# The end of a causal depthwise convolution: how many taps are left over before the last group's input, and how the last group's 31 taps are shared among four engines

## The chip, the core and the metric

The kernel runs on one core of a Trainium2 chip. A core has five engines that run their own instruction queues in order and meet at semaphores: TensorE (PE, with its weight loads PEld), VectorE (DVE), ScalarE (ACT), GpSimd (POOL) and SyncE (SP), which here issues the loads. The metric is the device time of one execution in microseconds, the median of several runs; beside it stands one execution that the hardware profiler recorded, with start and length of every instruction.

## The reference

The kernel computes a trunk of two layers on 256 tokens of width 2048, in float32. Layer 0 mixes tokens with a convolution module, layer 1 with latent attention; each is followed by a squared-ReLU MLP of width 8192. The change lies in the convolution module alone:

```python
def conv_module(h, w_pw1, b_pw1, w_dw, b_dw, ln_g, ln_b, w_pw2, b_pw2):
    u = h @ w_pw1 + b_pw1
    a, gate = jnp.split(u, 2, axis=-1)
    u = a * jax.nn.sigmoid(gate)
    u = lax.conv_general_dilated(          # depthwise, causal, width 31
        u, w_dw[:, None, :].astype(u.dtype), window_strides=(1,),
        padding=[(CONV_WIDTH - 1, 0)],
        dimension_numbers=("NWC", "WIO", "NWC"),
        feature_group_count=D_MODEL) + b_dw
    u = jax.nn.silu(layer_norm(u, ln_g, ln_b))
    return u @ w_pw2 + b_pw2
```

The depthwise convolution is, for each of the 2048 channels, a sum of 31 products: tap `w` is the channel's weight `w_dw[w]` times the gated input shifted by `w` tokens. The LayerNorm behind it needs all channels of a token, so nothing of the second projection can start before the last channel's sum is done.

## The kernel before

The 2048 channels are worked in 16 groups (`KC`) of 128, group `c` from 0 to 15. A group's gated input is a tile of 128 channels by 256 tokens with 30 zeros ahead (`ub`).

**One step of the loop.** A written-out loop (`for c in range(1, KC + 1)`) holds the order; the program says in which order each engine gets its instructions. In step `c` PE works on the first projection for group `c` (`conv_mm`, three passes of split float32), while the other engines finish group `c - 1`: `glu(c - 1)` forms the gated input from the projection's two accumulators, `start_sum` begins its sum of taps, `dve_taps` works through taps, `side_sum` adds up side products. Weights are split into a high and a low part by `conv_half(n, h)`: ACT writes `hi` (L173), and GpSimd or DVE writes `lo` (L174) from it; piece `n` of the weights has two halves. `conv_load` issues the load of a piece on SP's queue; there are three raw buffers, and a load waits until both halves of the piece three before it are split.

**Who computes a tap.** A tap can be done in three ways:
- DVE: one fused multiply and add onto an accumulator in PSUM (`dve_tap`, L978).
- Side tap: ACT multiplies (`product`, L898), GpSimd adds the products up in a tree (`side_sum`, L954), and DVE adds the tree's result to the accumulator (the join, an entry `None` in the list, L961).
- PE, in the last two groups only: ACT writes a diagonal matrix of the tap's 128 weights (`diag`, L907), and PE multiplies it by the shifted input (`last_products`, L918; `but_one_products`, L926 for group 14). `LAST_PE` taps of group 15 are done so, in two halves, eight of group 14.

**Leftovers.** `left[c]` is the list of a group's DVE taps that are not yet done. `dve_taps(c)` takes taps, oldest group first and in turn from two groups, until the number left over all groups is down to `rest(c)`: `REST` in general, `LAST_REST` for groups 13, 14 and 15. The taps left over are done in the next step. In the last step (`c == KC`, group 15) nothing may be left. Group 15's gated input `ub` is written by DVE itself (L888), and so stands in DVE's queue behind the taps of `dve_taps(14)`.

**The last step.** PE: the eight products of group 14, the first half of `last_products`, the transposes of group 13 to token order (`to_tokens`, L1016, which `dve_taps` issues when group 13's last tap has been issued), the second half, eight warm-up transposes (`keep_warm`, L238), the transposes of groups 14 and 15, 26 more warm-up transposes. DVE: the remaining taps; `half` (L972), the last tap of groups 14 and 15; `ca` (L975), which adds PE's part to `half`. `fill` holds the two statistics of groups 12 and 13 (`ln_stats`, L1026), put between the taps once `n` has reached `FILL_AT[1]` = 15 in the last step, otherwise behind them. Then: statistics of groups 14 and 15, mean and variance, reciprocal root (`rsqrt`, L221 to L226, whose square root runs on ACT), normalisation (L1159), swish and the second projection.

**Buffers.** The diagonals have `LAST_PE` buffers of 128 floats a partition, the side products `sum(LAST_SIDE)` buffers of 256.

Of the kernel before, what the change touches and what calls it, by code (L numbers as in the profile page):

```python
# [20 lines left out]
KC = D // P  # L21
# [23 lines left out]
PAD_O = 16  # L45
WB = 6
LOOK = WB // 2 - 1
LAST_PE = 22
BUT_ONE_PE = 8
SIDE = 2  # L50
LAST_SIDE = (3, 6, 4)
JOIN = 14
LEAD = 7
REST = (16, 18, 22)
LAST_REST = (20, 9, 0)
FILL_AT = (5, 15)
ORDERS = "STSTSTOSTSTSTSTT", "TSTSTSTOSTSTSTST"
N_S, N_G = 9, 2
# [28 lines left out]
def trunk_kernel(  # L87
# [55 lines left out]
    def nm(s):  # L143
        uid[0] += 1
        return f"{s}_{uid[0]}"


    def acc_tile():
        return psum["acc"].tile([P, NB], F32, tag="acc", name=nm("acc"))
# [17 lines left out]
    def split_half(raw, h, eng):  # L167

        _, nj, cols = raw.shape
        js = slice(h * nj // 2, (h + 1) * nj // 2)  # L170
        hi = wpool.tile([P, nj // 2, cols], F32R, tag="hi", name=nm("hi"), bufs=WB)
        lo = wpool.tile([P, nj // 2, cols], F32R, tag="lo", name=nm("lo"), bufs=WB)
        nc.scalar.activation(hi, raw[:, js, :], AF.Copy)  # L173
        eng.tensor_tensor(lo, raw[:, js, :], hi.bitcast(F32), op=ALU.subtract)  # L174
        return hi, lo
# [628 lines left out]
    with ExitStack() as cx:  # L804
# [30 lines left out]
        def conv_load(n):  # L835
            if n < NU:
                c, k = n // UC, n % UC * 8
                raws[n] = load(
                    [rows(conv_w_pw1[0], k, 8, c * P, P), rows(conv_w_pw1[0], k, 8, D + c * P, P)], 8
                )  # L840
            elif n < NU + KC // 2:
                raws[n] = load([rows(conv_w_pw2[0], 2 * (n - NU), 2, 0, 2 * NB)], 2)

        def conv_half(n, h):
            if n < NU + KC // 2:
                wjs[n, h] = split_half(raws[n], h, nc.gpsimd if 0 < n + h and (n, h) < (NU + 1, 1) else nc.vector)
# [20 lines left out]
        pss, ubs, pcs, cas, cts, sides, left = {}, {}, {}, {}, {}, {}, {}  # L867
        rest = lambda c: LAST_REST[c - KC + 3] if c > KC - 4 else REST[min(c, 2)]
        n_side = lambda c: LAST_SIDE[c - KC + 3] if c > KC - 4 else SIDE
        tap = lambda c, w: w_dw[:, w * KC + c : w * KC + c + 1]  # L870
# [9 lines left out]
        def glu(c):  # L880
            ub = ubs[c] = cv2.tile([P, PAD + S], F32, tag="ub", name=nm("ub"), bufs=3)
            (nc.vector if c == KC - 1 else nc.gpsimd).memset(ub[:, 0:PAD], 0.0)
            sg = cv2.tile([P, S], F32, tag="sg", name=nm("sg"), bufs=1)
            va, ga = pss.pop(c)
            nc.scalar.activation(sg, ga[:, :S], AF.Sigmoid, bias=b_pw1[:, KC + c : KC + c + 1])
            if c == KC - 1:

                nc.vector.scalar_tensor_tensor(  # L888
                    out=ub[:, PAD:], in0=va[:, :S], scalar=b_pw1[:, c : c + 1], in1=sg, op0=ALU.add, op1=ALU.mult
                )  # L890
            else:
                vb = cv2.tile([P, S], F32, tag="vb", name=nm("vb"), bufs=1)
                nc.scalar.activation(vb, va[:, :S], AF.Identity, bias=b_pw1[:, c : c + 1])
                nc.gpsimd.tensor_tensor(ub[:, PAD:], vb, sg, op=ALU.mult)

        def product(c, w):
            pr = cv2.tile([P, S], F32, tag="tp", name=nm("tp"), bufs=sum(LAST_SIDE))
            nc.scalar.activation(pr, ubs[c][:, w : w + S], AF.Copy, scale=tap(c, w))  # L898
            return pr

        def diag(c, w):
            if c == KC - 2:
                t, j = divmod(w - W + BUT_ONE_PE, 4)
                dg = cn[:, t, (KC - 4 + j) * P : (KC - 3 + j) * P]
            else:
                dg = cv2.tile([P, P], F32, tag="dg", name=nm("dg"), bufs=LAST_PE)
            nc.scalar.activation(dg, ident, AF.Copy, scale=tap(c, w))  # L907
            return dg
# [7 lines left out]
        def last_products(w0, w1):  # L916
            for w in range(w0, w1):
                nc.tensor.matmul(  # L918
                    last_sum[0], dgs[w], ubs[KC - 1][:, w : w + S], start=w == 0, stop=w == LAST_PE - 1
                )  # L920

        def but_one_products():
            but_one_sum.append(acc_tile()[:, :S])
            for i, dg in enumerate(but_one):
                w = W - BUT_ONE_PE + i
                nc.tensor.matmul(  # L926
                    but_one_sum[0], dg, ubs[KC - 2][:, w : w + S], start=i == 0, stop=i == BUT_ONE_PE - 1
                )

        def start_sum(c):  # L930
# [7 lines left out]
            else:  # L938
                pcs[c] = acc_tile()[:, :S]
                o = sum_tile()[:, :S]  # L940
                last_sum.append(o)
                last_products(0, LAST_PE // 2)
                w = LAST_PE
            n = n_side(c)
# [4 lines left out]
        def side_sum(c):  # L949
            ps = sides[c]  # L950
            step = 1
            while step < len(ps):
                for i in range(0, len(ps) - step, 2 * step):
                    nc.gpsimd.tensor_tensor(ps[i], ps[i], ps[i + step], op=ALU.add)  # L954
                step *= 2

        def dve_tap(c):
            w = left[c].pop(0)
            out = pcs[c]
            if w is None:  # L960
                nc.vector.tensor_tensor(out, out, sides[c][0], op=ALU.add)  # L961
                return
            if c == KC - 1 and w == LAST_PE + n_side(c):
                nc.vector.tensor_scalar(
# [17 lines left out]
        def dve_taps(c, fill):  # L982
# [4 lines left out]
            while sum(len(v) for v in left.values()) > rest(c):  # L987
# [12 lines left out]
                if c == KC - 1 and k == KC - 3 and not left[k]:  # L1000

                    to_tokens(k)
                    last_products(LAST_PE // 2, LAST_PE)
                last = turns["last"] = k
# [4 lines left out]
        def to_tokens(c):  # L1009

            if c % 2 == 0:
                cts[c // 2] = acc_tile() if c == KC - 2 else tr_tile()
            ct = cts[c // 2]
            for t in range(T):
                q = 2 * t + c % 2
                nc.tensor.transpose(  # L1016
                    ct[:, q * P : (q + 1) * P], ca_part(c)[:, t * P : (t + 1) * P], ident
                )

        def ln_stats(c):  # L1020
            fill = []
            if c % 2 == 1:
                ct = cts[c // 2]
                for t in range(T):
                    fill.append(
                        lambda t=t: nc.vector.bn_stats(stats[:, t, c // 2, :], ct[:, t * S : (t + 1) * S])  # L1026
                    )
                fill.append(lambda: nc.scalar.activation(
                    cn[:, :, (c - 1) * P : (c + 1) * P], ct.rearrange("p (t n) -> p t n", t=T), AF.Copy
                ))  # L1030
            return fill
# [11 lines left out]
        with tc.manual_schedule():  # L1043
# [57 lines left out]
            for c in range(1, KC + 1):  # L1101
                n = UC * c
                conv_load(n + 3)
                if c == KC:
                    but_one_products()
                glu(c - 1)
                fill = ln_stats(c - 4 if c < KC else KC - 3) if c > 3 else []
                fill, copies = fill[:T], fill[T:]
                if c < KC:
                    pss[c] = [acc_tile() for _ in range(2)]  # L1110
                conv_half(n + (c < KC), 0)
                start_sum(c - 1)
                if c < KC:
                    conv_half(n + 1, 1)
                    dve_taps(c - 1, fill)
                    conv_load(n + 4)
                    side_sum(c - 1)
                    conv_mm(c, 0, 8)
                    if c < KC - 1:
                        conv_half(n + 2, 0)  # L1120
                        conv_half(n + 2, 1)
                else:
                    side_sum(c - 1)
                    conv_half(n, 1)
                    conv_half(n + 1, 0)
                    dve_taps(c - 1, fill)
                    conv_load(n + 4)
                for f in copies:
                    f()
                if c < KC:  # L1130
                    conv_mm(c, 8)
                    if c > KC - 4:
                        dgs.extend(diag(KC - 1, w) for w in range(len(dgs), min(len(dgs) + 8, LAST_PE)))
                    if c == KC - 1:
                        but_one.extend(diag(KC - 2, w) for w in range(W - BUT_ONE_PE, W))
                    if c > 2:
                        to_tokens(c - 3)
                    conv_mm(c, 12)
# [139 lines left out]
    with ExitStack() as cx:  # L1278
# [322 lines left out]
        with tc.manual_schedule():  # L1601
# [89 lines left out]
            for g in range(NG):  # L1691
                for i in range(HG):
                    h = g * HG + i

                    n = -(-len(work) // (HG - i))
# [116 lines left out]
```

## Time and profile before

| what | value |
|---|---|
| median of 3 runs | 1931.16 us (1931.03 to 1931.22) |
| profiled execution, its own time | 1930.93 us |
| its span, first to last instruction | 1929.2 us |
| granted TensorE clock | 0.998 |
| busy: PE, DVE, ACT, POOL | 1904.2, 1647.4, 1208.2, 223.4 us |
| convolution's last two steps | about 190 to 217 us of the span |

In the profile, times are microseconds from the span's start. A row of a timeline has start, length, engine, line, operation, output and inputs with their shapes, the number of merged instructions, and in brackets the idle time of the engine ahead of it and who ended it. The lengths of neighbours on an engine overlap, so the step from one start to the next is what an instruction costs in a row of them. A row of the chain of waits has start, length and what the end of the program was waiting for then. `tr`, `acc` and `sum` are PSUM tiles; `tp` are side products, `dg` diagonals, `ca` a finished group.

### The profile page before, as it was taken

Reading aid. Unit: us, or ns where it says so; the run is one execution under the profiler, and the core shown is the slowest. Engines: PE = TensorE matmul, PEld = TensorE weight load, DVE = VectorE, ACT = ScalarE, POOL = GpSimd, SP = SyncE. Lnnn points to the kernel's source line nnn. Section 1 sums busy time; section 2 is a strip of 40 time slices with the busy share of each in tenths; the row PEclk is TensorE's granted clock in tenths of the full one; section 3 lists DMA queues with packets and bytes.
Section 4 is the critical chain, followed back from the end, with each engine's and each line's share of the span. In section 5 each row is a group of like instructions: output and inputs, shape, how many; then the busy total and the mean of one; then the engine's idle time right before and its main releaser. Section 6 shows DMA issues by size and latency. Waiting matters only on the chain.

```text
span 1929.2 us, 28511 instructions
## 1 busy us (share of the span) xinstructions
PE 1904.2 (99%) x10794; PEld 1669.2 (87%) x10794; DVE 1647.4 (85%) x2367; ACT 1208.2 (63%) x1717; POOL 223.4 (12%) x183
## 2 busy tenths in 40 slices
PE   7999999999999999999999999999999999999998
PEld 7999888888888888888899998888888888888886
DVE  5999865789999999999976665657999999999887
ACT  5556664766666666666566665566666666666654
POOL 5999300000000000000001410000000000000000
PEclk9999999999999999999999999999999999999999
DMA  8676365857666667666646445765667666766663
GB/s 236 187 195 179 129 196 154 234 172 206 203 201 206 197 202 213 200 200 212 205 143 182 118 151 175 205 188 173 199 193 210 208 197 197 217 201 197 212 220 109
DMA packets 407113, 367.62 MB, mean 191 GB/s; under 512 B 15416, under 2 KB 351936, under 8 KB 406720
## 3 DMA queue, kind: packets, MB, share of 16 engines
q1 hardware_dynamic: 405952, 363.63, 63.0%
q10 hardware_dynamic: 1024, 2.17, 0.3%
q8 instruction: 84, 1.38, 0.3%
q14 instruction: 53, 0.43, 0.1%
HBM read 363.68 MB, written 2.10 MB: 190 GB/s over the span
## 4 chain that ended last, share of the span: by engine, by line
PE 88%; DVE 9%; ACT 1%; POOL 1%; DMA 0%; issue 0%; SPq 0%; DVEq 0%; ACTq 0%; POOLq 0%
PE acc L520 24%; PE acc L199 15%; PE acc L200 15%; PE acc L201 15%; PE acc L518 12%; DVE sum L978 7%; PE acc L255 1%; PE sum L918 1%; ACT hi L173 0%; DMA xs<-in_x 0%; PE acc L863 0%; PE acc L864 0%; PE acc L865 0%; PE acc L1580 0%; PE acc L1444 0%
## 5 line engine op out<-in xcount | busy, mean ns | idle before, releaser
L431 DVE TENSOR_TENSOR lo<-raw,hi 128x1024 fp32r<-128x1024 f32 (+1 forms) x512 | 571.7, 1123 | 88.0 <-ACT hi L430 87.6
L430 ACT ACTIVATE hi<-raw 128x1024 fp32r<-128x1024 f32 (+1 forms) x512 | 480.0, 971 | 66.0 <-PE acc L200 65.8
L520 PE MATMUL acc<-xt,hi 128*128 128x512 f32 x2048 | 504.0, 391 | 0.0
L520 PEld LDWEIGHTS acc<-xt,hi 128*128 128x128 f32 x2048 | 374.8, 188 | 72.8 <-ACT hi L430 0.2
L199 PE MATMUL acc<-hi,sh 128*128 128x512 f32 x930 | 362.7, 390 | 0.0
L201 PE MATMUL acc<-lo,sh 128*128 128x512 f32 x930 | 361.9, 389 | 0.0
L200 PE MATMUL acc<-hi,sl 128*128 128x512 f32 x802 | 312.0, 389 | 0.0
L518 PEld LDWEIGHTS acc<-xt,lo 128*128 128x128 f32 x2048 | 257.7, 188 | 10.9
L518 PE MATMUL acc<-xt,lo 128*128 128x256 f32 x2048 | 259.7, 279 | 0.0
L173 ACT ACTIVATE hi<-raw 128x1024 fp32r<-128x1024 f32 (+2 forms) x184 | 180.1, 1006 | 46.2 <-PE acc L200 43.3
L201 PEld LDWEIGHTS acc<-lo,sh 128*128 128x128 f32 x930 | 174.5, 188 | 36.3
L199 PEld LDWEIGHTS acc<-hi,sh 128*128 128x128 f32 x930 | 174.6, 188 | 35.9
L174 DVE TENSOR_TENSOR lo<-raw,hi 128x1024 fp32r<-128x1024 f32 (+2 forms) x118 | 132.9, 1146 | 68.3 <-ACT hi L173 62.3
L430 ACT ACTIVATE hi<-V 128x1024 fp32r<-128x1024 f32 x94 | 99.6, 1060 | 130.7 <-DVE V L726 121.7
L200 PEld LDWEIGHTS acc<-hi,sl 128*128 128x128 f32 x802 | 150.5, 188 | 31.3
L978 DVE SCALAR_TENSOR_TENSOR sum<-ub,w_dw,sum 128x256 f32<-128x256 f32 x392 | 160.0, 512 | 6.4 <-ACT sum L934 5.5
L174 POOL TENSOR_TENSOR lo<-raw,hi 128x1024 fp32r<-128x1024 f32 x66 | 157.7, 2407 | 23.7 <-ACT hi L173 23.1
L430 ACT ACTIVATE hi<-T 128x1024 fp32r<-128x1024 f32 x94 | 99.5, 1058 | 92.5 <-DVE T L714 68.9
L525 ACT ACTIVATE U<-acc 128x512 f32<-128x512 f32 x128 | 75.9, 593 | 108.6 <-PE acc L520 108.6
L863 PE MATMUL acc<-xt,hi 128*128 128x256 f32 x512 | 143.6, 280 | 0.0
L865 PE MATMUL acc<-xt,lo 128*128 128x256 f32 x512 | 142.2, 278 | 0.6 <-POOL lo L174 0.6
L864 PE MATMUL acc<-xt,hi 128*128 128x256 f32 x512 | 142.2, 278 | 0.0
(275 smaller groups left out, 2810.4 us busy)
## 6 DMA issues: line engine op xcount, KB each, us to landing
raw<-in_mlp_w SPq DMA_DIRECT2D x256, 1024.0 KB, 6.2
raw<-in_conv_w_pw SPq DMA_DIRECT2D x64, 512.0 KB, 5.5
raw<-in_conv_w_pw SPq DMA_DIRECT2D x16, 1024.0 KB, 5.0
raw<-in_mla_w_o SPq DMA_DIRECT2D x16, 1024.0 KB, 5.5
raw<-in_mla_w_kv_up SPq DMA_DIRECT2D x8, 1024.0 KB, 5.6
raw<-in_mla_w_in SPq DMA_DIRECT2D x8, 576.0 KB, 3.8
raw<-in_mla_w_in SPq DMA_DIRECT2D x4, 1024.0 KB, 6.0
raw<-in_mla_w_q_up SPq DMA_DIRECT2D x16, 256.0 KB, 3.8
```

The lines of the kernel that those rows point to most:

```text
L173: nc.scalar.activation(hi, raw[:, js, :], AF.Copy)
L174: eng.tensor_tensor(lo, raw[:, js, :], hi.bitcast(F32), op=ALU.subtract)
L199: nc.tensor.matmul(ps, sh, mh, start=start, stop=False)
L200: nc.tensor.matmul(ps, sl, mh, start=False, stop=False)
L201: nc.tensor.matmul(ps, sh, ml, start=False, stop=stop)
L430: nc.scalar.activation(parts[0], src, AF.Copy)
L431: nc.vector.tensor_tensor(parts[1], src, parts[0].bitcast(F32), op=ALU.subtract)
L518: nc.tensor.matmul(ps[0][:, :S], wl[:, j, :], xh(k), start=False, stop=False)
L520: nc.tensor.matmul(ps[0], wh[:, j, :], xhl(k), start=k == 0, stop=k == KC - 1)
L863: nc.tensor.matmul(o, wh[:, bs], xh(k), start=k == 0, stop=False)
L864: nc.tensor.matmul(o, wh[:, bs], xl(k), start=False, stop=False)
L978: nc.vector.scalar_tensor_tensor(out=out, in0=ubs[c][:, w : w + S], scalar=tap(c, w), in1=pcs[c], op0=ALU.mult, op1=ALU.add)
```

## The change

Three numbers and the place of one call change:
- `LAST_PE` 22 to 18: PE does 18 of group 15's taps.
- `LAST_SIDE[2]` 4 to 6: six of group 15's taps go through ACT and GpSimd. DVE is left with 31 - 18 - 6 = 7 and the join, where it had 31 - 22 - 4 = 5 and the join.
- `LAST_REST[1]` 9 to 16: `dve_taps(14)` stops with 16 entries left over instead of 9.
- In the last step the first `conv_half(n, 0)`, a split of a piece of the second projection's weights, moves from ahead of `start_sum` to behind `side_sum`. In the other steps the call stays where it was.

```diff
-LAST_PE = 22
+LAST_PE = 18
 BUT_ONE_PE = 8
 SIDE = 2
-LAST_SIDE = (3, 6, 4)
+LAST_SIDE = (3, 6, 6)
 JOIN = 14
 LEAD = 7
 REST = (16, 18, 22)
-LAST_REST = (20, 9, 0)
+LAST_REST = (20, 16, 0)
 FILL_AT = (5, 15)
...
-                conv_half(n + (c < KC), 0)
+                if c < KC:
+                    conv_half(n + 1, 0)
                 start_sum(c - 1)
                 if c < KC:
                     conv_half(n + 1, 1)
...
                 else:
                     side_sum(c - 1)
+                    conv_half(n, 0)
                     conv_half(n, 1)
                     conv_half(n + 1, 0)
                     dve_taps(c - 1, fill)
```

The buffers of the diagonals go from 22 to 18, those of the side products from 13 to 15.

## The prediction

> **What bounds the kernel now.** I read the page first: its head, the engines' busy time and the chain that ended last.
>
> ```profile
> span 1929.2 us, 28511 instructions
> ...
> PE 1904.2 (99%) x10794; PEld 1669.2 (87%) x10794; DVE 1647.4 (85%) x2367; ACT 1208.2 (63%) x1717; POOL 223.4 (12%) x183
> ...
> PE 88%; DVE 9%; ACT 1%; POOL 1%; DMA 0%; issue 0%; SPq 0%; DVEq 0%; ACTq 0%; POOLq 0%
> ```
>
> TensorE (PE) carries 88% of the chain. DVE has 9%, nearly all of it in the convolution, where the taps (`dve_tap`, L978) set the pace. The change edits only the last two of the convolution's 16 channel groups, so next comes the chain of waits there, in order of time (start, us, what):
>
> ```profile
> 197.09 8.24 DVE sum L978 x21
> 205.33 0.41 DVE ub L888
> ...
> 205.78 5.02 PE sum L918 x22
> 210.80 0.22 PE tr L1016 x2
> 211.02 4.75 PE sum L918 x22
> 215.77 0.87 PE acc L238 x8
> 216.64 0.45 PE acc L1016 x4
> ...
> 217.12 0.76 DVE stats L1026 x2
> ...
> 218.79 0.49 ACT cn L1028
> ```
>
> Until 205.3 the chain is DVE's taps of groups 13 and 14. Behind them in DVE's queue stands `ub` of group 15 (L888), which everything of the last group needs. Then PE's 22 diagonal products (two instructions each, in halves of 22, the transposes of group 13 between them) run to 215.77; then come warm-up transposes (L238), the transposes of groups 14 and 15, the LayerNorm statistics, the root on ScalarE (ACT), and the second projection. The timelines of DVE and PE tell how much room each has:
>
> ```profile
> 205.21 0.51 DVE L888 SCALAR_TENSOR_TENSOR ub<-acc,vecs_cv,sg 128x256 f32<-128x256 f32 x1
> ...
> 205.58 1.33 DVE L978 SCALAR_TENSOR_TENSOR sum<-ub,w_dw,sum 128x256 f32<-128x256 f32 x3
> ...
> 207.53 0.61 DVE L964 TENSOR_SCALAR acc<-ub,w_dw,vecs_cv 128x256 f32<-128x256 f32 x1
> 207.98 0.55 DVE L978 SCALAR_TENSOR_TENSOR sum<-ub,w_dw,sum 128x256 f32<-128x256 f32 x1
> ...
> 210.27 0.55 DVE L972 SCALAR_TENSOR_TENSOR half<-ub,w_dw,sum 128x256 f32<-128x256 f32 x1
> 210.91 0.42 DVE L975 TENSOR_TENSOR ca<-acc,half 128x256 f32<-128x256 f32 x1
> ...
> 211.59 0.42 DVE L1026 BATCH_NORM_STATS2 stats<-tr 128x6 f32<-128x256 f32 x1
> 211.93 0.46 DVE L972 SCALAR_TENSOR_TENSOR half<-ub,w_dw,acc 128x256 f32<-128x256 f32 x1
> 215.81 0.42 DVE L975 TENSOR_TENSOR ca<-sum,half 128x256 f32<-128x256 f32 x1 [3.42 <-PE sum L918]
> ```
> ```profile
> 201.31 3.61 PE L926 MATMUL acc<-ub,cn 128*128 128x256 f32 x16
> 205.78 5.02 PE L918 MATMUL sum<-ub,dg 128*128 128x256 f32 x22 [0.86 <-DVE ub L888]
> ```
>
> So PE waits 0.86 for `ub` at 205, and DVE waits 3.42 for PE at the end of the group. The two are out of balance by that much, and the change shifts work from PE to DVE.
>
> **The change part by part.**
>
> *16 taps left over instead of 9.* Seven taps of groups 13 and 14 move from before `ub` to behind it. 21 alternating taps take 8.24 us in the chain, 0.393 each; `ub` comes 7 x 0.393 = 2.75 earlier, its start at 202.46. What else it needs is there: the gate's sigmoid starts at 201.57 (row below) and lasts 0.47. PE cannot take all of this: its 16 products of group 14 run from 201.31, 3.61 long, to 204.92. An L918 starts every (210.63 - 205.78) / 22 = 0.22 us, the end of one overlapping the next, so without the wait the next starts at about 204.8. PE gains 0.9 to 1.0 there; the other 1.8 of the 2.75 is hidden behind PE.
>
> *18 taps on PE instead of 22.* Four products, eight instructions of 0.22, fall away: 1.76 us, four in each half. First half 204.8 + 18 x 0.22 = 208.77; transposes of group 13 start there; second half from 208.99 to 213.0, against 215.7. PE's part shrinks by 2.7. The four diagonals that ACT no longer makes were ahead of the sigmoid:
>
> ```profile
> 197.24 1.85 ACT L907 ACTIVATE dg<-ident,w_dw 128x128 f32<-128x128 f32 x6
> ...
> 201.57 0.47 ACT L885 ACTIVATE sg<-acc,vecs_cv 128x256 f32<-128x256 f32 x1
> ...
> 205.76 1.71 ACT L898 ACTIVATE tp<-ub,w_dw 128x256 f32<-128x256 f32 x4 [2.77 <-DVE ub L888]
> ...
> 216.69 0.60 ACT L1028 ACTIVATE cn<-tr 128x512 f32<-128x512 f32 x1 [7.32 <-DVE stats L1026]
> 217.29 1.28 ACT L232 ACT_TABLE_LOAD   x1
> ```
>
> That is 1.2 us of ACT, but the sigmoid waits for PE's last gated product (201.31 is where PE goes on to L926), so it is worth 0 to 0.1; I take 0.
>
> *Six side taps on ACT and GpSimd, and the weight split (`conv_half(n, 0)`) behind them.* `ub` ends at 202.97. Six products at 0.42 (the L898 row: four in 1.71) end at 205.6. GpSimd (POOL) now has five additions instead of three, and the moved half's conversion comes after them:
>
> ```profile
> 203.07 2.35 POOL L174 TENSOR_TENSOR lo<-raw,hi 128x1024 fp32r<-128x1024 f32 x1 [0.84 <-ACT hi L173]
> 206.75 2.33 POOL L954 TENSOR_TENSOR tp<-tp,tp 128x256 f32<-128x256 f32 x3 [1.33 <-ACT tp L898]
> 209.04 4.67 POOL L174 TENSOR_TENSOR lo<-raw,hi 128x1024 fp32r<-128x1024 f32 x2
> ```
>
> The additions start 1.0 behind `ub` as here, at 204.0, at 0.75 to 0.8 each with the waits for products: last one done at 207.9. DVE's join wants it at 213.4 (below), so that costs nothing; without that cover each late us would be one us at the end. Then three conversions at 2.34: 210.2, 212.5, 214.9 (before: 213.7). All feed the second projection, which begins behind 218: hidden. The second frees a buffer for a 1 MB load on SP's queue, 1.1 later than now; at the page's 5.0 us it lands near 217.6, and ACT converts that piece from about 229:
>
> ```profile
> raw<-in_conv_w_pw SPq DMA_DIRECT2D x16, 1024.0 KB, 5.0
> ```
> ```profile
> 231.75 2.00 ACT L173 ACTIVATE hi<-raw 128x1024 fp32r<-128x1024 f32 x2
> ```
>
> The load after it moves likewise; both stay hidden with over 10 us. The order of the loads on SP does not change.
>
> *What DVE has behind `ub`.* Seven moved taps bring it to 205.57, exactly where the first tap of the last round stood before (205.58). From there it does what it did, plus group 15's two extra taps (7 instead of 5). The rule in `dve_taps` changes the order: the two statistics of groups 12 and 13 are put in after 15 taps, and the list ends with group 15 alone: tap, tap, join, tap. Three things cost here:
> - The first tap starts 0.37 behind `ub` (205.21 to 205.58), at 202.83; 14 steps of 0.393 and one of 0.45 (207.53 to 207.98) bring the statistics to 208.78. But PE transposes group 13 only at 208.77, for 0.38. DVE stands until 209.19, some 0.4. Queued behind are all the remaining taps.
> - Both statistics now lie ahead of the end; the second (0.34, from 211.59 to 211.93) used to come after it.
> - Steps in a row on one accumulator are slower. The opening of the convolution, with one group at work, shows it: the row below is followed by the join at 42.42, so 14 taps in 7.42, 0.53 each, against 0.393 alternating.
>
> ```profile
> 35.00 7.32 DVE L978 SCALAR_TENSOR_TENSOR sum<-ub,w_dw,sum 128x256 f32<-128x256 f32 x14 [4.37 <-ACT sum L934]
> 42.42 0.43 DVE L961 TENSOR_TENSOR sum<-sum,tp 128x256 f32<-128x256 f32 x1
> ```
>
> A rule bears on this. The Trainium skill, "VectorE: DVE Perf Modes", section "The DRAIN you can't avoid", has it that a chain of VectorE operations costs the same with a semaphore after each as with one at the end. By that the last steps would cost 0.39 each, and the sum below would be 0.4 better, a gain of 2.7. The trace disagrees (0.53 against 0.393), and the measurement decides.
>
> In time: statistics 209.19, join of 14 209.53, statistics 209.86, then 15, 14, 15 at 210.20, 210.59, 210.99, `half` of 14 at 211.38, its `ca` 0.64 later (as 210.27 to 210.91) at 212.02, group 15's taps at 212.37 and 212.90, join 213.43, `half` 0.47 later at 213.90, `ca` of 15 at 214.54. PE was done at 213.1. So DVE ends the group, 1.27 earlier than 215.81, and PE becomes the one with room.
>
> *Behind it.* The eight warm-up transposes and those of group 14 now fit into PE's waiting: 213.0 to 214.3. Group 15's two follow `ca` (ends 214.96) at 215.0, take 0.38, and the statistics start at 215.40 instead of 217.12: 1.72 earlier. One more wait shrinks. The root on ACT stood behind the table load of 217.29, `warm` and the copy of 218.79, all held back by the late statistics of groups 12 and 13:
>
> ```profile
> 218.41 0.17 DVE L221 TENSOR_SCALAR v<-mv 128x2 f32<-128x2 f32 x1
> 219.40 0.17 DVE L223 RECIPROCAL y<-t 128x2 f32<-128x2 f32 x1 [0.81 <-ACT t L222]
> ```
>
> With those statistics at 209.9, table and `warm` are done by 212.5. The copy of groups 14 and 15 starts at 216.2 and is out of the way by 216.7; `v` ends at 216.87, the root returns 0.25 later, `y` starts at 217.12 instead of 219.40. That 0.56 is bounded by 0 (if the copy comes late) and 0.6; I take 0.56, since the copy's own time is in the rows. Nothing further changes in length: the gain at `y` is 2.28. PE's 26 warm-up transposes (3.00) start at 215.2 and end at 218.2; the first normalised tile is there at 218.4, so PE's wait for it shrinks from 0.74 but does not vanish. From there PE is full, so the gain passes to the end:
>
> ```profile
> 216.92 3.00 PE L238 MATMUL acc<-ident 128*128 128x128 f32 x26
> 220.65 1.52 PE L1169 MATMUL acc<-ident,cn 128*128 128x128 f32 x8 [0.74 <-DVE cn L1159]
> ```
> ```profile
> 225.00:260.00 35.00, 35.00 (x165) 28.89 (x164) 27.30 (x37) 24.06 (x33) 0.00 (x0) 1.00 0.56 181
> ```
>
> In that last row, of the stretch 225 to 260, the first busy time is PE's: 35.00 of 35, at a granted clock of 1.00.
>
> Sum: 1.27 + 0.45 (transposes and warm-up taken out) + 0.56 = 2.28. The profiled execution had 1930.93 (span 1929.2), the runs' median is 1931.16, 0.23 more; from the median 1928.9, the new span near 1926.9.
>
> **The rivals.**
> - *PE ends the group, not DVE.* If the last taps overlap as alternating ones and the turned group is there in time, PE's end 2.7 earlier carries all behind it along, with the 0.56 a gain of 3.2, 1927.9. For it: DVE's end is only 1.4 behind PE's. Against it: the 0.53.
> - *The gain is given back.* DVE's end comes later than worked out: the wait for group 13's transposes grows from 0.43 to 1.4 if PE still starts at 205.78, or tap and join slow down. 1930.4 to 1931.6. Against it: nothing in the rows keeps PE past 204.92.
> - *GpSimd blocks DVE, and it gets slower.* POOL ends at 214.9, 1.8 before DVE's first SBUF-only operations of the LayerNorm (`v`, now 216.7). From 1.8 us of delay on POOL, a conversion could hold DVE for up to its 2.35: the gain is gone with one, and 1931.2 to 1933.6 results with two. Against it: the 21 taps from 197.09 keep their 0.393 beside POOL's conversion of 203.07. The Trainium skill, "SBUF — State Buffer", section "SBUF: two separate sides", speaks of an exclusive port pair that VectorE's two-port modes and GpSimd lock for whole instructions; no row here shows such a hold, since the taps read one operand from PSUM.
> - *Something no row shows.* The buffers of diagonals and side products change in number (22 to 18 of 512 bytes a partition, 13 to 15 of 1024, the same in sum), so addresses within move by 2 KB. If this or another effect changes each tap a little, it reaches beyond 4 us either way.
>
> **How the numbers follow.** 0.65 for the forecast, own range 1928.2 to 1929.6 (the bounds of the 0.56, the 0.43 and the 0.4); 0.11 for PE ending the group; 0.07 for the gain given back; 0.04 for GpSimd; 0.13 for what no row shows, 0.08 of it faster by more than 3.9 us, 0.05 slower. 0.2% (3.9 us) is about what a measurement of this kernel can tell from no change, and the forecast of 0.12% lies within it: faster 0.08, same 0.87, slower 0.05. The range 1927.7 to 1931.1 takes in the forecast, the first rival and most of the second.
>
> **What would show it.** `ub` near 202.5 and no wait of the first L918 for it; 36 L918 instead of 44; a wait of some 0.4 of L1026 for PE; L975 of group 15 no longer waiting 3.42 for PE but near 214.5, PE waiting about 0.7 for `ca`; the first L223 near 217.1. Wrong would make it: L918 still starting near 205.8, the last `ca` waiting for PE or GpSimd, POOL still converting at 216.7, or a tap rate other than 0.393.

## The result and the profile after

The changed kernel takes 1928.61 us (median of 20 runs, 1928.18 to 1930.15) against 1931.13 of before (20 runs): 2.5 us less, a ratio of 0.9987 with a 95% interval of 0.9981 to 0.9992. It is faster by 0.13%, inside the 0.2% that the prediction named as the limit of what a measurement can tell; with 20 runs of each kernel the interval leaves out a ratio of 1 all the same. The first profiled execution of it (1930.15 us, span 1928.4) reached PE's products of group 14 already 1.3 us late. That delay builds up between about 46 and 80 us, long ahead of the last step: GpSimd's conversions start at 46.16 and 80.03 there, at 45.64 and 78.85 in the second profiled execution. So the lines here are of that second one, span 1926.5, in which the products of group 14 start at 201.33 as they did before (201.31).

The chain of waits of the changed kernel, over the last step:

```profile
201.49 3.45 PE acc L926 x16
204.94 3.89 PE sum L918 x18
208.83 0.23 PE tr L1016 x2
...
209.44 0.42 DVE sum L961
...
211.77 0.42 DVE ca L975
...
213.22 0.45 DVE acc L961
...
213.69 0.49 DVE half L972
...
214.27 0.43 DVE ca L975
...
214.75 0.45 PE acc L1016 x2
...
215.23 0.76 DVE stats L1026 x2
...
216.53 0.18 DVE v L221
216.73 0.21 ACT t L222
216.97 0.18 DVE y L223
```

Two things differ from before. The chain no longer runs through DVE's taps and `ub` into the first diagonal product: PE goes from group 14's products (L926) to group 15's (L918) without a wait. And it changes engine in the middle of the step: after the transposes of group 13 it is DVE's, to `ca` of group 15 at 214.27 and beyond. Timeline of PE and of DVE, changed kernel:

```profile
204.78 4.05 PE L918 MATMUL sum<-ub,dg 128*128 128x256 f32 x18
208.67 0.38 PE L1016 MATMUL tr<-ident,ca 128*128 128x128 f32 x2
208.88 4.05 PE L918 MATMUL sum<-ub,dg 128*128 128x256 f32 x18
212.78 1.04 PE L238 MATMUL acc<-ident 128*128 128x128 f32 x8
213.65 0.38 PE L1016 MATMUL acc<-ident,ca 128*128 128x128 f32 x2
214.75 0.44 PE L1016 MATMUL acc<-ident,ca 128*128 128x128 f32 x2 [0.72 <-DVE ca L975]
```
```profile
202.59 0.44 DVE L888 SCALAR_TENSOR_TENSOR ub<-acc,vecs_cv,sg 128x256 f32<-128x256 f32 x1
...
208.50 0.47 DVE L978 SCALAR_TENSOR_TENSOR acc<-ub,w_dw,acc 128x256 f32<-128x256 f32 x1
209.09 0.43 DVE L1026 BATCH_NORM_STATS2 stats<-tr 128x6 f32<-128x256 f32 x1
...
214.27 0.42 DVE L975 TENSOR_TENSOR ca<-sum,half 128x256 f32<-128x256 f32 x1
...
216.53 0.17 DVE L221 TENSOR_SCALAR v<-mv 128x2 f32<-128x2 f32 x1
216.97 0.17 DVE L223 RECIPROCAL y<-t 128x2 f32<-128x2 f32 x1 [0.27 <-ACT t L222]
```

`ub` comes at 202.59; the first L918 at 204.78 has no bracket, where it had waited 0.86. There are 36 of them. PE is through with them at 212.78 and later waits 0.72 for `ca`, while `ca` no longer waits 3.42 for PE. The step from `v` (the variance plus a small constant, L221) to `y` (the reciprocal of its root, L223), with the root on ACT between them, is 0.44 long (216.53 to 216.97), against 0.99 before.

### The profile page after: what moved, and what is told of

Read it like the earlier page. It is cut to its first block, busy times and chain, and to the rows that moved or that the text cites. A ratio compares the mean times of both kernels' runs of the same rounds, so it can differ in the third digit from the quotient of the medians.

```text
span 1928.4 us, 28496 instructions
## 1 busy us (share of the span) xinstructions
PE 1903.1 (99%) x10786; PEld 1668.2 (87%) x10786; DVE 1648.2 (85%) x2369; ACT 1206.5 (63%) x1715; POOL 224.9 (12%) x185
## 3 DMA queue, kind: packets, MB, share of 16 engines
q8 instruction: 84, 1.38, 0.3%
## 4 chain that ended last, share of the span: by engine, by line
PE 88%; DVE 9%; ACT 1%; DMA 1%; POOL 1%; issue 0%; DVEq 0%; ACTq 0%
PE acc L520 24%; PE acc L199 15%; PE acc L200 15%; PE acc L201 15%; PE acc L518 12%; DVE sum L978 7%; PE acc L255 1%; PE acc L865 0%; PE acc L864 0%; PE acc L863 0%; ACT hi L173 0%; PE acc L1582 0%; DMA xs<-in_x 0%; PE acc L1446 0%; PE acc L1447 0%
## 5 line engine op out<-in xcount | busy, mean ns | idle before, releaser
L518 PEld LDWEIGHTS acc<-xt,lo 128*128 128x128 f32 x2048 | 257.7, 188 | 10.9
L518 PE MATMUL acc<-xt,lo 128*128 128x256 f32 x2048 | 259.8, 279 | 0.0
```

Of the source, the lines that this page charges most:

```text
L518: nc.tensor.matmul(ps[0][:, :S], wl[:, j, :], xh(k), start=False, stop=False)
```

## The experiments

Each was timed against the kernel before on the same chip; three chips were used, on which the median of before was 1931.06, 1931.01 and 1931.07. Gains are differences of medians; the ratios' intervals are about 0.0009 wide to each side (1.7 us), so the gains are read together with the lines of each profile, and the starts on the engines decide. Medians of the changed kernel are 1928.56 and 1928.61.

### The changed kernel again

No edit.

> The changed kernel once more, for a profile without the late start of the first one. Theory (DVE ends the group): 2.3 to 2.5 us below before; counted from PE's first L926, ub near 1.2, first L918 near 3.5, L1026 waiting 0.2 to 0.4 for the transposes of group 13, ca of group 15 near 13.2, first L223 near 15.8 (before: 3.9, 4.5, 14.5, 18.1). Rival (PE ends the group): ca of group 15 near 11.9.

Measured 1928.56 (ratio 0.9987, 0.9978 to 0.9996). Counted from the first L926 (201.33): `ub` 1.26, L918 3.45, `ca` of group 15 12.94, L223 15.64. DVE ends the group.

### Leftover alone

```diff
-LAST_REST = (20, 9, 0)
+LAST_REST = (20, 16, 0)
```

> Before with 16 instead of 9 left over, nothing else. Theory: ub comes 2.75 earlier, PE takes 0.95 of it, and with 22 products still ends the group at about 214.85 instead of 215.81; the statistics of groups 12 and 13 now lie between the taps, behind a wait of about 1.3 for PE's transposes, so the root on ACT is no longer held up: 0.95 + 0.56 = 1.5 us faster than before. Rival (the root's wait does not shrink): 0.95. Rival (nothing of the 2.75 is hidden behind PE): 2.75 or more.

Measured 1929.41 us against 1931.06: 1.65 faster, ratio 0.9991 (0.9983 to 1.0). DVE's timeline of this kernel:

```profile
202.49 0.45 DVE L888 SCALAR_TENSOR_TENSOR ub<-acc,vecs_cv,sg 128x256 f32<-128x256 f32 x1
...
209.85 0.43 DVE L1026 BATCH_NORM_STATS2 stats<-tr 128x6 f32<-128x256 f32 x1 [0.98 <-PE tr L1016]
...
214.60 0.42 DVE L975 TENSOR_TENSOR ca<-sum,half 128x256 f32<-128x256 f32 x1 [0.79 <-PE sum L918]
...
217.66 0.17 DVE L223 RECIPROCAL y<-t 128x2 f32<-128x2 f32 x1 [0.27 <-ACT t L222]
```

`ub` is as early as in the change, and `ca` still waits for PE: of the 2.7 that `ub` gains, the group's end gains 1.13 (`ca` 13.37 behind the first L926, which starts at 201.23 here, against 14.50). The first L918 gains 1.02 of it (3.45 behind the first L926 against 4.47), about what was expected. The rest of the 1.65 is the shorter wait for the root (0.27 instead of 0.81).

### Sharing alone

```diff
-LAST_PE = 22
+LAST_PE = 18
...
-LAST_SIDE = (3, 6, 4)
+LAST_SIDE = (3, 6, 6)
```

> Before with 18 taps on PE and six side taps, still 9 left over and the weight split where it was. Theory: ub and the first L918 stay at 205.2 and 205.8; eight L918 fewer end PE at 214.05 and DVE is done before, so PE ends the group 1.7 earlier, and with the statistics put between the taps the root's wait shrinks by 0.56: 2.3 us faster, as much as the whole change. Rival (earlier ub is what the change lives from): under 1.5.

Measured 1928.78: 2.28 faster, ratio 0.9988 (0.9979 to 0.9997). DVE's timeline:

```profile
205.32 0.52 DVE L888 SCALAR_TENSOR_TENSOR ub<-acc,vecs_cv,sg 128x256 f32<-128x256 f32 x1
...
213.27 0.48 DVE L972 SCALAR_TENSOR_TENSOR half<-ub,w_dw,acc 128x256 f32<-128x256 f32 x1
214.19 0.42 DVE L975 TENSOR_TENSOR ca<-sum,half 128x256 f32<-128x256 f32 x1 [0.44 <-PE sum L918]
...
217.24 0.17 DVE L223 RECIPROCAL y<-t 128x2 f32<-128x2 f32 x1 [0.27 <-ACT t L222]
```

`ub` is as late as before, and still this half of the change gives 2.28 of the whole one's 2.50. The two halves give 1.65 and 2.28, together not 3.93 but 2.50. Both contain the root's 0.55, which can be had once. What is left of each, 1.1 and 1.7, comes from an earlier end of PE's part: the first half starts it earlier, the second makes it shorter. With both, PE is through 2.85 earlier than before (11.45 behind the first L926 against 14.30), but then DVE is last, and what PE gains beyond is lost.

An earlier `ub` does not bring DVE's own end forward, since it only moves taps of DVE from ahead of `ub` to behind it. Here, with `ub` 2.7 later than in the change, `half` of group 15 starts 11.87 behind the first L926; in the change it starts 12.36 behind it. The difference goes with the statistics of groups 12 and 13: here they start at 211.75 and 212.48, between group 15's last taps, in the change at 209.09 and 209.76, the first behind a wait. The next experiment moves them alone.

### The statistics between the last taps

```diff
-FILL_AT = (5, 15)
+FILL_AT = (5, 99)
```

on the changed kernel.

> The change with FILL_AT[1] = 99: the two statistics of groups 12 and 13 then come between group 15's last taps, where no other group is left. Theory: DVE no longer waits 0.2 to 0.4 for the transposes, and each statistic stands between two steps on one accumulator, which then cost no 0.53: ca of group 15 comes 0.5 to 0.7 earlier than in the change, 2.8 to 3.0 us faster than before. Rival (PE ends the group already): no difference from the change. Rival by the rule that a chain costs the same with and without semaphores: only the wait is won, 0.2 to 0.4.

Measured 1928.12: 2.94 faster than before, 0.44 faster than the change; ratio 0.9985 (0.9976 to 0.9994). DVE's timeline:

```profile
211.40 0.48 DVE L978 SCALAR_TENSOR_TENSOR acc<-ub,w_dw,acc 128x256 f32<-128x256 f32 x1
211.78 0.43 DVE L1026 BATCH_NORM_STATS2 stats<-tr 128x6 f32<-128x256 f32 x1
212.12 0.47 DVE L978 SCALAR_TENSOR_TENSOR acc<-ub,w_dw,acc 128x256 f32<-128x256 f32 x1
212.51 0.42 DVE L1026 BATCH_NORM_STATS2 stats<-tr 128x6 f32<-128x256 f32 x1
212.85 0.41 DVE L961 TENSOR_TENSOR acc<-acc,tp 128x256 f32<-128x256 f32 x1
213.30 0.48 DVE L972 SCALAR_TENSOR_TENSOR half<-ub,w_dw,acc 128x256 f32<-128x256 f32 x1
213.88 0.42 DVE L975 TENSOR_TENSOR ca<-sum,half 128x256 f32<-128x256 f32 x1
```

From tap to join, with both statistics between, it takes 1.45 (211.40 to 212.85). In the change the same two taps take 1.11 up to the join (212.11 to 213.22), and the statistics 0.69 elsewhere, behind a wait of 0.2. So between two steps on one accumulator the two statistics cost 0.34 instead of 0.69: the 0.53 of such steps is partly waiting, which other work can fill. `half` of group 15 is back at 11.85 behind the first L926, where it was in sharing alone. The Trainium skill, "VectorE: DVE Perf Modes", section "The DRAIN you can't avoid", has it that a chain costs the same with and without a semaphore after each operation. Read as the prediction read it, as one price for every step, that would have left only the wait of 0.2 to be won; against this reading stands that `ca` comes 0.5 earlier counted from the first L926 (12.43 against 12.94). The section compares copies with and without semaphores and does not speak of neighbours that share an accumulator, so it is the reading that fails here, not what was measured there.

### Twelve left over

```diff
-LAST_REST = (20, 16, 0)
+LAST_REST = (20, 12, 0)
```

on the changed kernel.

> The change with 12 instead of 16 left over. Theory (of the 2.75 that ub comes earlier, PE can use 0.95 only): ub comes 1.57 later than in the change, ends 0.2 ahead of the end of group 14's products, and the first L918 stays where it is; the statistics of groups 12 and 13 fall four taps later and DVE no longer waits for the transposes: 0.1 to 0.3 faster than the change. Rival (an earlier ub is worth something in itself, to the side taps or to PE): slower than the change by 0.5 to 1.5.

Measured 1928.25: 2.76 faster than before; ratio 0.9986 (0.9977 to 0.9995). DVE's timeline:

```profile
204.07 0.44 DVE L888 SCALAR_TENSOR_TENSOR ub<-acc,vecs_cv,sg 128x256 f32<-128x256 f32 x1
```

`ub` starts 1.5 later than in the change, and the first L918 at 204.73 against 204.78. These 1.5 us of an earlier `ub` are worth nothing. What differs is where the statistics fall: the first comes at 210.31, well behind the transposes of 208.62, and up to `ca` DVE waits for nothing. Counted from the first L926, `ca` of group 15 comes 0.25 earlier than in the change (12.69 against 12.94).

### The weight split in its old place

```diff
-                if c < KC:
-                    conv_half(n + 1, 0)
+                conv_half(n + (c < KC), 0)
                 start_sum(c - 1)
...
                     side_sum(c - 1)
-                    conv_half(n, 0)
                     conv_half(n, 1)
```

on the changed kernel.

> The change with the weight split of the last step back ahead of start_sum. Theory: ACT's 1.05 for it lies in the wait for ub, GpSimd's conversion delays the five additions by 1.2 to 1.5, done near 209.4, and DVE's join asks for them only at 213.2: no difference from the change (within 0.15). Rival (the side sum comes late): slower by what L961 of group 15 waits, up to 1.

Measured 1928.65, ratio 0.9988 (0.9979 to 0.9997): no difference from the change. From the first L926 to the first L223 it takes 15.63, in the change 15.64 (its profiled execution, 1930.3 us, starts the last step as late as the changed kernel's first one: L926 at 202.75). The moved call is worth nothing by itself.

### GpSimd kept busy longer

```diff
-nc.gpsimd if 0 < n + h and (n, h) < (NU + 1, 1) else nc.vector
+nc.gpsimd if 0 < n + h and (n, h) < (NU + 2, 1) else nc.vector
...
                     conv_half(n + 1, 0)
+                    conv_half(n + 1, 1)
+                    conv_half(n + 2, 0)
                     dve_taps(c - 1, fill)
```

on the changed kernel; the two halves are no longer converted in the projection.

> The change with two more halves of the second projection's weights converted in the last step on GpSimd (DVE converts them in the projection otherwise), so that GpSimd works until about 219.5, over DVE's v, reciprocal root and first normalisation (216.5 to 219.8). Theory: these keep their lengths and starts, no difference from the change (within 0.2). Rival (GpSimd's conversions and DVE's operations within SBUF hold each other off): v or L1161 wait up to 2.3, or GpSimd's conversions grow from 2.34 by as much; slower than the change by 0.5 to 2.3.

Measured 1931.49: 2.9 slower than the change; against before 1.0003 (0.9994 to 1.0011). The theory was wrong here and its rival right in kind, though the loss is more than its 2.3. Timelines of GpSimd, of DVE and of PE:

```profile
207.84 11.64 POOL L174 TENSOR_TENSOR lo<-raw,hi 128x1024 fp32r<-128x1024 f32 x5
```
```profile
216.59 0.62 DVE L221 TENSOR_SCALAR v<-mv 128x2 f32<-128x2 f32 x1
217.47 0.17 DVE L223 RECIPROCAL y<-t 128x2 f32<-128x2 f32 x1 [0.27 <-ACT t L222]
217.67 1.82 DVE L224 SCALAR_TENSOR_TENSOR t<-y 128x2 f32<-128x2 f32 x1
219.53 0.16 DVE L225 TENSOR_TENSOR t<-t,v 128x2 f32<-128x2 f32 x1
```
```profile
220.39 1.52 PE L1173 MATMUL acc<-ident,cn 128*128 128x128 f32 x8 [2.30 <-DVE cn L1163]
```

GpSimd is busy to 219.48. Two DVE operations on two numbers a partition, 0.17 long otherwise, take 0.62 and 1.82. The second ends at 219.49, with GpSimd's last conversion. The first ends at 217.21; the fourth of five conversions, at 2.33 each, ends at 207.84 + 9.3 = 217.2. So each is held until the conversion that is under way ends. The hold accounts for 2.1: PE's first L1173 (the normalised tiles' transposes) starts 2.1 later than in the change, both counted from the first L926. The two profiled executions differ by 2.6 (1930.91 against 1928.32); near 319 us, at PE's first L518, it is 2.2, and the remaining 0.4 lies behind and was not located. The medians differ by more, 2.9, because the runs of this kernel fall into two groups: five at 1930.5 to 1930.9, the profiled one among them, and six at 1931.5 to 1933.1. What the second group adds was not recorded.

### One conversion more on GpSimd

As the last, with `(NU + 2, 0)` and only the first of the two added lines.

> The change with one more half (not two) converted on GpSimd in the last step, so that GpSimd ends near 217.2. Theory after the run with two (a GpSimd conversion holds DVE's operations within SBUF): v starts at 216.5 and ends only with that conversion, 0.6 long instead of 0.17; L224, behind it, keeps its 0.16, since GpSimd is done; slower than the change by 0.4 to 0.6. Rival (the loss in the run with two came from the weights' changed places in the projection): v keeps 0.17, and the loss, if any, lies behind 223.

Measured 1929.15: 0.55 to 0.6 slower than the change; ratio to before 0.9991 (0.9982 to 0.9999). Timelines of GpSimd and DVE:

```profile
207.81 9.33 POOL L174 TENSOR_TENSOR lo<-raw,hi 128x1024 fp32r<-128x1024 f32 x4
```
```profile
216.55 0.62 DVE L221 TENSOR_SCALAR v<-mv 128x2 f32<-128x2 f32 x1
217.44 0.17 DVE L223 RECIPROCAL y<-t 128x2 f32<-128x2 f32 x1 [0.27 <-ACT t L222]
217.64 0.16 DVE L224 SCALAR_TENSOR_TENSOR t<-y 128x2 f32<-128x2 f32 x1
```

GpSimd ends at 217.14 and `v` at 217.17, and L224, later than that, is as short as ever. Counted from the first L926, `y` comes 0.45 later than in the change (16.09 against 15.64), as much as `v` is held. The hold goes with GpSimd's end, not with where the weights are converted.

### Nine side taps

```diff
-LAST_PE = 18
+LAST_PE = 17
...
-LAST_SIDE = (3, 6, 6)
+LAST_SIDE = (3, 6, 9)
...
-FILL_AT = (5, 15)
+FILL_AT = (5, 19)
...
-name=nm("tp"), bufs=sum(LAST_SIDE))
+name=nm("tp"), bufs=15)
```

on the changed kernel.

> The change with 17 taps on PE, nine side taps (in the same 15 buffers), five on DVE, and FILL_AT[1] = 19, so that the two statistics come after 19 and 20 steps. Theory (behind the change DVE ends the group, and GpSimd has five us of room): nine products end near 207.0, eight additions near 210.2, DVE's join asks at 212.1; DVE ends at 213.0, PE at 212.7, the statistics of groups 14 and 15 start near 214.2: 3.4 to 3.6 faster than before. Rival (GpSimd ends the group): join waits, 2.5 or less. Rival (GpSimd's conversions, now until 217.2, hold DVE off): 2 or less.

Measured 1930.3 (1928.72 to 1930.84): 0.7 faster than before, slower than the change; ratio 0.9996 (0.9987 to 1.0005). Timelines of GpSimd and DVE (this execution has the late start of the changed kernel's first one: L926 at 202.56, 1.2 late):

```profile
204.83 6.12 POOL L954 TENSOR_TENSOR tp<-tp,tp 128x256 f32<-128x256 f32 x8 [1.35 <-ACT tp L898]
210.91 7.00 POOL L174 TENSOR_TENSOR lo<-raw,hi 128x1024 fp32r<-128x1024 f32 x3
```
```profile
212.68 0.42 DVE L961 TENSOR_TENSOR acc<-acc,tp 128x256 f32<-128x256 f32 x1
...
213.78 0.43 DVE L975 TENSOR_TENSOR ca<-sum,half 128x256 f32<-128x256 f32 x1 [0.16 <-PE sum L918]
...
216.39 1.55 DVE L221 TENSOR_SCALAR v<-mv 128x2 f32<-128x2 f32 x1
```

The taps do what was expected: the join does not wait for GpSimd, and `ca` comes 11.22 behind the first L926 against 12.94 in the change. (`ub`, at 203.33, is only 0.7 late here, which flatters DVE; in the next experiment, without the late start, `ca` is at 11.57.) But GpSimd's conversions now end at 217.91, and `v` is held for 1.4, until 217.94. What the sums gained is lost a few instructions later.

### Nine side taps, and GpSimd done in time

```diff
-nc.gpsimd if 0 < n + h and (n, h) < (NU + 1, 1) else nc.vector
+nc.gpsimd if 0 < n + h and (n, h) < (NU + 1, 0) else nc.vector
...
                     conv_half(n, 1)
-                    conv_half(n + 1, 0)
                     dve_taps(c - 1, fill)
...
                     if m == 0 and j == 0:
+                        conv_half(NU + 1, 0)
                         conv_half(NU + 1, 1)
```

on the kernel with nine side taps.

> 17 on PE, nine side taps, five on DVE, and the second weight piece's first half no longer on GpSimd in the last step but on DVE in the projection. GpSimd then ends near 214.9, v starts at 215.2 to 215.5. Theory (the hold was all that the nine side taps lost by): 3.3 to 3.6 us faster than before. Rival (something else in nine side taps costs): under 2.5.

Measured 1927.31 (1927.01 to 1927.61): 3.76 faster than before, a little more than expected; ratio 0.998 (0.9971 to 0.9989). Timelines of GpSimd and DVE:

```profile
210.19 4.68 POOL L174 TENSOR_TENSOR lo<-raw,hi 128x1024 fp32r<-128x1024 f32 x2
```
```profile
212.99 0.42 DVE L975 TENSOR_TENSOR ca<-sum,half 128x256 f32<-128x256 f32 x1
...
215.24 0.17 DVE L221 TENSOR_SCALAR v<-mv 128x2 f32<-128x2 f32 x1
215.68 0.17 DVE L223 RECIPROCAL y<-t 128x2 f32<-128x2 f32 x1 [0.27 <-ACT t L222]
```

GpSimd ends at 214.87, `v` starts at 215.24 and is 0.17 long again. With one conversion moved from GpSimd to DVE the median falls by 3.0 us (1930.30 to 1927.31). Not all of this is the hold. The two profiled executions differ by as much (1930.17 and 1927.15), and there it can be divided: 1.14 lies ahead of the first L926 (202.56 and 201.42), the late start; 1.38 lies between it and PE's first normalised tile (16.90 and 15.52 behind it), the hold; 0.5 lies behind. The fastest run with nine side taps, 1928.72, is 1.4 above this kernel's median. How many of the other runs started late was not recorded, nor whether the moved conversion has to do with it. So it is shown that the hold cost 1.4 in the profiled execution, and not that it was all that the nine side taps lost by.

### And the weight split in its old place

Both edits of "The weight split in its old place", on the kernel just told of.

> The same with the last step's first weight split back ahead of start_sum, so that GpSimd converts it while DVE still writes ub, and ends near 213.9, 1.5 ahead of v; the additions end near 211.6, and the join asks at 212.1. Theory: 3.3 to 3.6 us faster than before, with less spread than the same kernel without this. Rival (the join waits for GpSimd): L961 of group 15 waits, 2.5 to 3.2.

Measured 1927.22 (1927.0 to 1928.85): 3.85 faster than before, ratio 0.9982 (0.9973 to 0.999). GpSimd ends at 213.56, `v` starts at 215.21; the join does not wait. It is not measurably faster than the last one, and the spread is not smaller (the last one's runs lie between 1927.01 and 1927.61): that part of the expectation failed. These two are the fastest kernels of the study.

## Why the prediction was right, point by point

Predicted were 2.28 us; the runs show 2.5. The forecast mechanism, DVE ending the group, is what the profile shows. The named range, 1927.7 to 1931.1, reaches almost to the time of before, so it says little that the time lies in it; the forecast starts inside the step say more, and they held to within 0.3.

In the prediction's own terms, 1.27 + 0.45 + 0.56 = 2.28 became 1.54 + 0.35 + 0.55 = 2.44: `ca` of group 15 came 1.54 earlier than before (215.81 to 214.27), the way from there to the statistics shrank by 0.35 (from 1.31 to 0.96), and the root's wait by 0.55. At `y` the profiles differ by 2.43 (219.40 to 216.97). Two of the terms missed in opposite directions, so that the sum came out better than its largest term.

- *Leftover.* `ub` at 202.59 (predicted 202.46), first L918 at 204.78 (204.8), second half done and warm-up begun at 212.78 (213.0 in one sentence of the prediction, 213.1 in another). That most of the earlier `ub` is hidden behind PE is shown by the runs with 12 left over (1.5 less of it, no L918 later) and with leftover alone.
- *Sharing.* GpSimd's five additions end at 207.87 (predicted 207.9), its conversions at 214.82 (214.9); the join did not wait.
- *The wait for group 13's transposes* was sized at some 0.4 and was 0.2 (208.50 + 0.39 to 209.09): the transposes came 0.1 earlier and the taps 0.1 later than taken. The wait therefore ended only 0.1 earlier than forecast.
- *`half` to `ca`* was taken as 0.64 from group 14's pair before; in the changed kernel it is 0.51 for group 14 (211.26 to 211.77) and 0.58 for group 15. That is 0.13 and 0.06. With the 0.10 of the wait it makes 0.29; group 15's two taps took 0.05 of it back (1.11 to the join against 1.06), and with roundings this is the 0.27 by which `ca` came earlier than forecast (214.27 against 214.54).
- *From `ca` to the statistics* the forecast had 0.86 (214.54 to 215.40); it was 0.96 (214.27 to 215.23). Group 15's transposes took 0.44 and not 0.38, and the statistics came 0.48 behind their start and not 0.40. This took back 0.1 of the 0.27.
- *The root.* Taken as 0.56, measured 0.55 (0.99 less 0.44). Every kernel here whose statistics of groups 12 and 13 stand ahead of the end has the 0.27 in L223's bracket, leftover alone as well as sharing alone: the gain goes with their place, which each half of the change moves. That it needs nothing else is argued from the order of ACT's queue in the prediction's rows; no run moved the statistics alone on the kernel before.
- *`y`* at 216.97 against 217.12, PE's first normalised tile at 218.23 against 218.4. From there the gain was passed on: PE's first L518 starts at 316.75, before at 319.22, 2.47 earlier.
- *The moved split* was costed at nothing, and that is what it is.
- *Rivals.* PE ending the group was as far off as forecast: PE was done 1.5 ahead. That the gain would be given back did not happen.
- *GpSimd holding DVE* did not happen in the changed kernel, since GpSimd ends at 214.82 and `v` starts at 216.53, 1.7 later (1.8 in the forecast). But the hold exists, and the forecast's reason against it went too far: that the taps keep their 0.393 beside GpSimd's conversions says nothing of operations whose operands all lie in SBUF. The bound of up to 2.35 for one conversion was the right size (0.45, 1.4 and 1.65 seen). The rule of the Trainium skill on an exclusive port pair, "SBUF — State Buffer", section "SBUF: two separate sides", names the VectorE operations that are held beside GpSimd: those in a two-port mode, and those with two inputs in SBUF if GpSimd's operation reads SBUF. L224, with two inputs in SBUF, is held (1.82), and the taps, with one of two in PSUM, are not (0.393): both agree. `v` has one input and is held too; no row shows in which mode it ran.
- *Something no row shows* was not seen: the taps' steps are 0.393 in all kernels.

## What to carry to other kernels

Take two engines that wait for each other in turn: list what each still has to do behind the common start, find which ends last, and expect two remedies that both bring the same engine's end forward not to add up (1.65 and 2.28 made 2.50). Look at the small serial work behind the join too: a fifth of the gain here came from statistics that stood earlier in a queue, so that a copy and a table load on another engine were out of the way. And when work is handed to GpSimd because it is idle, check what VectorE does within SBUF at the time when GpSimd's queue will now end.

## What the runs showed of the hardware that was not expected

- A GpSimd conversion of 128x1024 (2.33 us) holds some VectorE operations whose operands lie in SBUF until it ends: L221, 0.17 alone, took 0.62, 0.62 and 1.55, and L224, 0.16 alone, took 1.82. Not all: the reciprocal L223 stayed at 0.17 at 217.47, while a conversion ran to 219.48, and so did the aggregation L1150 and its like at 0.58 ahead of `v`. Why these two are free was not tried.
- After such a hold VectorE's operation goes in between two conversions of GpSimd's queue: with two conversions left, `v` was held by the first only, and L224 by the second.
- Over the last step, the rows of the taps are 0.46 to 0.50 us long in most of these profiles and 0.53 to 0.55 in that of before and of sharing alone, at the same step of 0.393; with the longer rows, `half` to `ca` of group 14 is 0.64 to 0.65, with the shorter 0.5 to 0.6. What sets this was not found.
- Three of the profiled executions (the changed kernel's first, the weight split in its old place, nine side taps) reach the first L926 1.2 to 1.4 us late, the others between 201.23 and 201.45. In these three GpSimd's conversions are 0.4 to 0.5 late near 46 us and 1.0 to 1.2 near 79 us. What sets this off was not found.
